# Sharing the PSUM banks out anew for the neighborhood attention of a fused two-block network

## The chip, the cores and the metric

The kernel runs on one core of one Trainium2 chip. The metric is the device time of one execution in microseconds (us); lower is better. A figure given as "the time" is the median of several executions. The trace is of one further execution, taken by the hardware profiler.

The engines are named as in the profile: PE is TensorE (matmuls and transposes), PEld its weight loads, DVE is VectorE, ACT is ScalarE, POOL is GpSimd, SP is SyncE, which here issues the DMAs. PSUM, the memory that matmuls write to, has eight banks; a tile of 128 x 512 fp32 fills one.

## The reference, cut to what matters

The network has eight stages on 256 rows of 1024 features; the change touches the fifth, the "even" layer. Half of its mixer is a long convolution (hyena), the other half neighborhood attention (NA): 16 heads of width 32, in which each query sees a window of the 4 x 64 grid and all 256 context keys in one softmax. The concatenated halves go through one 1024 x 1024 product, the mixing product.

```python
h = modulate(rmsnorm(x, g_mix), sh1, sc1)
z = h @ w_in[i]
q, k, v = jnp.split(z[..., 3 * C_HYENA:], 3, axis=-1)
...
y_na = neighborhood_attention(to_grid(q, rows), to_grid(k, rows), to_grid(v, rows), kc, vc, na_rpb[i])
y_hy = hyena_mixer(z[..., :3 * C_HYENA], *hy)
x = x + gt1 * (jnp.concatenate([y_hy, y_na], axis=-1) @ w_mix_out[i])
...
x = x + gt2 * swiglu(modulate(rmsnorm(x, g_ffn), sh2, sc2), ffn_w1[i], ffn_w3[i], ffn_w2[i])
```

## The kernel before, in words

The stages run in the order ret, ffn0, dil, ffn1, even, ffn2, fou, moe. Within them the order of instructions on each engine is set by a scheduler when the program is built: it takes whatever is ready by its own model, earlier written code first, as far as tiles are free. On the chip each engine then runs its instructions strictly in that order and waits where an operand or a tile isn't ready. PSUM tiles come from one pool with three names: `mm` for products, `tp` for transposes, `aux` for the rest. `banks(mm, tp, aux)` says how many banks each has: 4, 2, 2 in this part.

Products are made in fp32 by splitting both operands in a high and a low part (`wh`, `wl`; `xTh`, `xTl`; `yTh`, `yTl`) and adding three matmuls. `load` fetches weights by DMA (L110) into one of three raw slots and converts each half of it with one ACT instruction (L119, high part) and one DVE instruction (L120, low part) into one of five slots `w`.

**Neighborhood attention** (`neighborhood`, L915 to L945) has four column groups c of four heads; each group has two pairs of heads (h0), each pair two blocks b of 128 queries. For one head and block: two score matmuls for the local keys and two for the context keys (L936, L937) into a tile S of `aux`; DVE adds the bias and takes the extremum (L394); ACT takes the exponential (L396); DVE the reciprocal and the scaling (L398, L399); PE transposes four times into a `tp` tile (L402); ACT copies it to P (L404); the pair's 16 value matmuls (L943) add into the group's tile O. At the end of a group O is split into `yT[4 + c]` (L149, L150). For each pair the bias tables are fetched anew (L927, SP) and masked (L928, DVE).

**The mixing product** (`down`, matmuls L197) has eight weight pieces g = 0 to 7 of 12 matmuls each, 128 x 512. Piece g multiplies `yT[g]`: pieces 0 to 3 are hyena's output, 4 to 7 that of NA's column groups 0 to 3. Pieces 0 to 2 are written one by one, 3 to 7 as one block, first for the first 128 rows and then for the others. Its four result tiles take all four `mm` banks.

**Behind it** `gated_residual` multiplies the result by a row `grow`, which a DMA brings (L562), and adds x (L672, L673: DVE). Then `norm_mod` scales each block of 128 rows by its root mean square (L578, L579, L218 on POOL, L593), transposes it in two sets of four into `tp` tiles (L596), modulates them (L604 on ACT, L607 on DVE) and splits them to `xTh`, `xTl` (L149, L150). The next stage's first matmuls are L176; its constants `csrh`, `csrl` are made from a DMA (L978) into a tile `n`, of the same slots as the norm's scaled rows.

Of the kernel before, what the change touches and what calls it, by code (L numbers as in the profile page):

```python
# [24 lines left out]
PSUM = bass.MemoryType.PSUM  # L25
# [27 lines left out]
class Net:  # L53
# [24 lines left out]
    def banks(s, mm, tp, aux):  # L78

        s.psx.close()  # L80
        s.ps, s.psn = s.pool("psum%d" % mm, 1, s.psx, space=PSUM), (mm, tp, aux)

    def mm_tile(s, shape, name="mm"):
        return s.ps.tile(shape, F32, name=name, tag="mm", bufs=s.psn[0])
# [322 lines left out]
    def dilated(s, x, xt):  # L407
        nc = s.nc
        with ExitStack() as ctx:
# [24 lines left out]
            for qd in range(4):  # L434
# [45 lines left out]
                nc.sync.dma_start(out=bias.rearrange("p h k c -> p (h k) c"), in_=src)  # L480
                O = s.mm_tile([128, 2, 256])

                for c in range(2):
                    for b in range(2):
# [9 lines left out]
                        for n, (g, kb) in enumerate(order):  # L494
                            for e in range(2):
                                hs = slice(64 * (2 * c + e), 64 * (2 * c + e) + 64)
                                nc.tensor.matmul(out=O[64 * e:64 * e + 64, c, b * 128:b * 128 + 128],
                                                 lhsT=V[g][:, kb, hs], rhs=P[e][:, n, :], start=n == 0, stop=n == 3)
                for c in range(2):
                    s.split(ot[0][:, 2 * qd + c, :].rearrange("p (a s) -> p s a", s=2),  # L500
                            ot[1][:, 2 * qd + c, :].rearrange("p (a s) -> p s a", s=2),
                            O[:, c, :].rearrange("p (s a) -> p s a", s=2))
            po = s.down(ot, "attn_w_out", 0, 8)
# [411 lines left out]
    def neighborhood(s, ctx, yt):  # L915
        nc = s.nc
        p = s.pool("na", 2, ctx)
        kt, vt, mask, biases, qps = s.na
        rpb = s.a["na_rpb"]
        for c in range(4):  # L920
            O = s.mm_tile([128, 256])
            for h0 in range(0, 4, 2):
                for hh, bt in enumerate(biases, h0):
                    for r2 in range(2):
                        src = bass.AP(tensor=rpb.tensor, offset=rpb.offset + (4 * c + hh) * 1905 + (5 - r2) * 127,
                                      ap=[[1, 64], [127, 6], [1, 64]])
                        nc.sync.dma_start(out=bt[64 - 64 * r2:128 - 64 * r2, 4:10, :], in_=src)  # L927
                    nc.vector.tensor_tensor(out=bt[:, 4:10, :], in0=bt[:, 4:10, :],  # L928
                                            in1=mask[:, None, :].to_broadcast([128, 6, 64]), op=ALU.add)

                for b in range(2):
                    P = []
                    for hh, bt in enumerate(biases, h0):
                        S = s.aux_tile([128, 2, 256])
                        q = qps[c // 2][:, c % 2, hh, b * 128:b * 128 + 128]
                        nc.tensor.matmul(out=S[:, b, :], lhsT=q, rhs=kt[:, c, :], start=True, stop=True)  # L936
                        nc.tensor.matmul(out=S[:, 1 - b, :], lhsT=q, rhs=s.kc[:, c, :], start=True, stop=True)  # L937
                        P.append(s.attend(p, S.rearrange("p n c -> p (n c)"),
                                          (bt[:, 6:14, :] if b == 0 else bt[:, 0:8, :]).rearrange("p m c -> p (m c)")))
                    vs = [vt, vt, s.vc, s.vc] if b == 0 else [s.vc, s.vc, vt, vt]  # L940
                    for n in range(4):
                        for i, hh in enumerate((h0, h0 + 1)):
                            nc.tensor.matmul(out=O[32 * hh:32 * hh + 32, b * 128:b * 128 + 128],  # L943
                                             lhsT=vs[n][:, n % 2, 128 * c + 32 * hh:128 * c + 32 * hh + 32],
                                             rhs=P[i][:, n, :], start=n == 0, stop=n == 3, tile_position=(0, 32 * hh))  # L945
            s.split(yt[0][:, 4 + c, :], yt[1][:, 4 + c, :], O)

    def even_layer(s, x, xt, then):
        with ExitStack() as ctx:
            keep = s.pool("even", 1, ctx)  # L950
            yt = s.pair(keep, [128, 8, 256], "yT")
            with ExitStack() as c2:
                fill = s.neighborhood_inputs(c2, xt)
                next(fill)
                s.hyena(c2, yt, xt, fill)
                for _ in fill:
                    pass
                s.neighborhood(c2, yt)
            grow = s.mod_row(s.pool("even_g", 1, ctx), 0, 2, "grow")
            po = s.down(yt, "w_mix_out", 0, 8)  # L960
            return s.gated_residual(x, po, grow, then)

    def ffn_second(s, x, xt, then):
        with ExitStack() as ctx:
# [658 lines left out]
```

## Time and profile before

| what | value |
|---|---|
| time, median of 3 runs | 2315.85 us (2314.77 to 2316.75) |
| the profiled execution's own time | 2317.26 us |
| its span, first to last instruction | 2315.2 us |
| busy share of the span: PE, PEld, DVE, ACT | 97%, 76%, 64%, 46% |
| mean granted clock of TensorE | 0.983 of 2.4 GHz |

A window row of the trace below gives the stretch and its length in us, then for PE, PEld, DVE, ACT and POOL the busy time with the number of instructions in brackets, then PEclk (the granted clock, 1.00 is 2.4 GHz), the mean busy share of the DMA engines, and GB/s. With the instructions of one line alone, it gives PE and PEld, PEclk, DMA share and GB/s. A timeline row gives start, duration, engine, line, operation, written tile <- read tiles, shape and count, and in brackets the idle time of the engine before it and what ended that.

### The profile page before, as it was taken

The numbers are of one execution on the slowest core, as the hardware profiler recorded it, in microseconds if no ns is written. First come the engines' busy times: TensorE is split into PE (matmuls) and PEld (weight loads), VectorE is DVE, ScalarE is ACT, GpSimd is POOL, SyncE is SP. The second block draws the span as 40 slices with busy tenths as digits, with TensorE's granted clock in tenths as the row PEclk, the third lists the DMA queues.
The fourth block names the chain that finished last, engine by engine and source line by source line (L and its number), as shares of the span: only waits on it lengthen the run. The fifth ranks groups of instructions, "written<-read, shape, count | busy, mean of one in ns | idle before, by whom it ended". The sixth has DMA issues, their size and how long they took to land. (4 is left out here: it accounts for less than half of the span.)

```text
span 2315.2 us, 34156 instructions
## 1 busy us (share of the span) xinstructions
PE 2236.4 (97%) x13729; PEld 1766.7 (76%) x13729; DVE 1486.4 (64%) x2024; ACT 1072.7 (46%) x1424; POOL 33.5 (1%) x39
## 2 busy tenths in 40 slices
PE   8999999999999999998899988999999999999997
PEld 8997998899997998986699877665566656656662
DVE  6987887867746655886655457555555655555553
ACT  4333444354445444645554345544444544444442
POOL 0000000000000000100000000000000000000000
PEclk9999999999999999999999997999999999999998
DMA  8666777777743555642355627899899989998994
GB/s 308 244 255 234 264 254 273 271 263 264 268 151 132 207 191 181 217 164 40 118 189 194 254 100 278 346 414 416 356 376 425 422 338 412 425 420 356 424 424 183
DMA packets 99712, 639.75 MB, mean 276 GB/s; under 512 B 22552, under 2 KB 33433, under 8 KB 39513
## 3 DMA queue, kind: packets, MB, share of 16 engines
q1 hardware_dynamic: 99128, 636.71, 71.6%
q8 instruction: 110, 1.80, 0.3%
q10 hardware_dynamic: 416, 0.78, 0.1%
q14 instruction: 58, 0.47, 0.1%
HBM read 634.17 MB, written 3.28 MB: 275 GB/s over the span
## 5 line engine op out<-in xcount | busy, mean ns | idle before, releaser
L119 ACT ACTIVATE wh<-raw 128x1024 fp32r<-128x1024 f32 x446 | 468.8, 1059 | 552.1 <-PE mm L160 256.8
L120 DVE TENSOR_TENSOR wl<-raw,wh 128x1024 fp32r<-128x1024 f32 x446 | 538.9, 1220 | 246.4 <-ACT wh L119 245.4
L160 PE MATMUL mm<-xTh,wh 128*128 128x256 f32 x1600 | 447.5, 280 | 0.7 <-ACT tm L825 0.7
L160 PE MATMUL mm<-xTh,wl 128*128 128x256 f32 x1600 | 446.5, 279 | 0.0
L160 PE MATMUL mm<-xTl,wh 128*128 128x256 f32 x1600 | 445.3, 278 | 0.0
L120 DVE TENSOR_TENSOR wl<-rawy,wh 128x1024 fp32r<-128x1024 f32 x216 | 255.6, 1222 | 87.1 <-ACT wh L119 86.5
L160 PEld LDWEIGHTS mm<-xTh,wh 128*128 128x128 f32 x1600 | 301.3, 188 | 7.7 <-issue 5.8
L160 PEld LDWEIGHTS mm<-xTh,wl 128*128 128x128 f32 x1600 | 300.8, 188 | 4.3 <-issue 4.3
L160 PEld LDWEIGHTS mm<-xTl,wh 128*128 128x128 f32 x1600 | 301.2, 188 | 3.3 <-issue 3.3
L119 ACT ACTIVATE wh<-rawy 128x1024 fp32r<-128x1024 f32 x216 | 224.1, 1057 | 52.3 <-PE mm L1079 27.9
L1067 PE MATMUL mm<-rawx,hx 128*64 128x512 f32 x864 | 202.7, 595 | 0.0
L1079 PE MATMUL mm<-wl,hgh 128*128 128x512 f32 x448 | 179.6, 402 | 4.1 <-DVE wl L120 4.1
L1079 PE MATMUL mm<-wh,hgh 128*128 128x512 f32 x448 | 181.1, 404 | 0.0
L1079 PE MATMUL mm<-wh,hgl 128*128 128x512 f32 x448 | 177.8, 397 | 0.0
L176 PE MATMUL mm<-wh,xTh 128*128 128x256 f32 x608 | 174.1, 288 | 2.8 <-ACT wh L119 2.4
L176 PE MATMUL mm<-wh,xTl 128*128 128x256 f32 x608 | 174.3, 287 | 1.5 <-DVE xTl L150 1.5
L176 PE MATMUL mm<-wl,xTh 128*128 128x256 f32 x608 | 173.9, 286 | 0.5 <-DVE wl L120 0.5
L1067 PEld LDWEIGHTS mm<-rawx,hx 128*64 128x64 f32 x864 | 62.3, 137 | 117.8 <-issue 117.3
L535 DVE CUSTOM_DVE_ANT_0 araw<-araw,cond 128x1024 f32<-128x1024 f32 x96 | 115.7, 1218 | 33.3 <-DMA araw<-in_w_ada_dram 33.2
L176 PEld LDWEIGHTS mm<-wh,xTh 128*128 128x128 f32 x608 | 118.3, 195 | 5.1 <-ACT wh L119 2.8
L176 PEld LDWEIGHTS mm<-wh,xTl 128*128 128x128 f32 x608 | 118.7, 195 | 2.8 <-DVE xTl L150 2.3
L176 PEld LDWEIGHTS mm<-wl,xTh 128*128 128x128 f32 x608 | 118.4, 195 | 1.5 <-DVE wl L120 1.0
(361 smaller groups left out, 3293.6 us busy)
## 6 DMA issues: line engine op xcount, KB each, us to landing
rawx<-in_moe_w_dram SPq DMA_DIRECT2D x56, 2048.0 KB, 11.3
rawy<-in_moe_w_dram SPq DMA_DIRECT2D x56, 2048.0 KB, 15.0
raw<-in_moe_w_dram SPq DMA_DIRECT2D x84, 1024.0 KB, 11.5
araw<-in_w_ada_dram SPq DMA_DIRECT2D x48, 1024.0 KB, 5.5
raw<-in_ffn_w_up_dram SPq DMA_DIRECT2D x44, 1024.0 KB, 4.8
raw<-in_attn_w_in_dram SPq DMA_DIRECT2D x36, 1024.0 KB, 5.0
raw<-in_ffn_w_dram SPq DMA_DIRECT2D x33, 1024.0 KB, 4.9
x<-in_moe_w_dram SPq DMA_DIRECT2D x28, 1024.0 KB, 8.2
```

The lines of the kernel that those rows point to most:

```text
L119: nc.scalar.activation(out=h, in_=v, func=AF.Copy)
L120: nc.vector.tensor_tensor(out=l, in0=v, in1=h.bitcast(F32), op=ALU.subtract)
L160: s.nc.tensor.matmul(out=p[:, j, :], lhsT=a[:, kc, :], rhs=b[:, kc, :], start=n == 0, stop=n == 23)
L176: s.nc.tensor.matmul(out=p[:, tb if to is None else to, :], lhsT=a[:, kc, tb, :], rhs=b[:, kc % 4, :], start=n == 0, stop=n == 23)
L535: nc.vector.tensor_tensor_reduce(out=out, in0=r[:, j, :], in1=cond[src], scale=1.0, scalar=0.0, op0=ALU.mult, op1=ALU.add, accum_out=dst)
L1067: nc.tensor.matmul(out=ps[half], lhsT=x[:, kc, :], rhs=w[:, kc, :], start=kc == 0, stop=kc == 7)
L1079: nc.tensor.matmul(out=pm, lhsT=a[:, kc, :], rhs=b[:, kc % 2, :], start=n == 0, stop=n == 23)
```

## The change

NA's result tile O is taken from `aux` and no longer from `mm`. Around NA, the mixing product, the residual and the norm behind it, the banks are 4 `mm`, 1 `tp`, 3 `aux`; then they are 4, 2, 2 again. The pool has one name wherever it is opened, and a new pool's tiles wait tile by tile for the old pool's readers in the same place. Lines up to 956 keep their numbers; those behind L960 are four higher.

```diff
     def banks(s, mm, tp, aux):

         s.psx.close()
-        s.ps, s.psn = s.pool("psum%d" % mm, 1, s.psx, space=PSUM), (mm, tp, aux)
+        s.ps, s.psn = s.pool("psum", 1, s.psx, space=PSUM, reuse_waits="tile"), (mm, tp, aux)
...
         for c in range(4):
-            O = s.mm_tile([128, 256])
+            O = s.aux_tile([128, 256])
             for h0 in range(0, 4, 2):
...
                 for _ in fill:
                     pass
+
+                s.banks(4, 1, 3)
                 s.neighborhood(c2, yt)
             grow = s.mod_row(s.pool("even_g", 1, ctx), 0, 2, "grow")
             po = s.down(yt, "w_mix_out", 0, 8)
-            return s.gated_residual(x, po, grow, then)
+            x = s.gated_residual(x, po, grow, then)
+            s.banks(4, 2, 2)
+            return x
```

The scheduler turns this into another order at three places.

The first is PE at the start of NA, column group 0. `nk`, `nq`, `kc` are keys, queries and context keys, `flip` the matrix that transposes, `nv`, `vc` the values. Before:

```order
L936 MATMUL aux<-nk,nq_9905 128x256
L402 MATMUL tp<-flip,L 128x128 x4
L937 MATMUL aux<-kc,nq_9905 128x256
L402 MATMUL tp<-flip,L 128x128 x4
L943 MATMUL mm<-P,nv 32x128
L402 MATMUL tp<-flip,L 128x128 x3
L943 MATMUL mm<-P,nv 32x128 x3
```

And now:

```order
L937 MATMUL aux<-kc,nq_9905 128x256
L197 MATMUL mm<-wh,yTh 128x512 x2
L197 MATMUL mm<-wh,yTl 128x512 x2
L197 MATMUL mm<-wl,yTh 128x512 x2
L197 MATMUL mm<-wh,yTh 128x512 x2
L197 MATMUL mm<-wh,yTl 128x512 x2
L197 MATMUL mm<-wl,yTh 128x512 x2
L197 MATMUL mm<-wh,yTh 128x512 x2
L402 MATMUL tp<-flip,L 128x128 x4
L197 MATMUL mm<-wh,yTl 128x512 x2
L197 MATMUL mm<-wl,yTh 128x512 x2
L197 MATMUL mm<-wh,yTh 128x512
```

Matmuls of the mixing product stand ahead of the first head's transposes. In all, 84 of its 96 stand ahead of NA's last L943 now (17 did): 48 (pieces 0 to 3) in column group 0, 12 in each of the groups 1, 2 and 3. There is one `tp` tile: a set of four transposes can't begin before the reader of the set ahead of it is done.

The second is PE at the end of the mixing product. `ident` is the identity, `n` the scaled rows. Before:

```order
L197 MATMUL mm<-wl,yTh 128x512 x2
L596 MATMUL tp<-ident,n 128x128 x8
L1216 MATMUL aux<-wb,ones 128x64
L596 MATMUL tp<-ident,n 128x128 x4
L176 MATMUL mm<-wh,xTh 128x256
L596 MATMUL tp<-ident,n 128x128 x4
L176 MATMUL mm<-wh,xTl 128x256
```

And now:

```order
L943 MATMUL aux<-P,nv 32x128 x4
L197 MATMUL mm<-wh,yTh 128x512 x3
L197 MATMUL mm<-wh,yTl 128x512 x2
L197 MATMUL mm<-wl,yTh 128x512 x2
L197 MATMUL mm<-wh,yTh 128x512
L197 MATMUL mm<-wh,yTl 128x512 x2
L197 MATMUL mm<-wl,yTh 128x512 x2
L596 MATMUL tp<-ident,n 128x128 x16
L176 MATMUL mm<-wh,xTh 128x256
```

Twelve L197 are left behind NA, and all 16 transposes of the norm stand ahead of the next stage's first matmul, through one `tp` tile.

The third is ACT in the norm behind it. `mod` is the modulation, `tm` its result. Before:

```order
L604 ACTIVATE tm<-tp,mod 128x128 x4
L149 ACTIVATE xTh<-tm 128x4x128 x2
L149 ACTIVATE csrh<-n 128x768 x2
```

And now:

```order
L604 ACTIVATE tm<-tp,mod 128x128 x2
L149 ACTIVATE xTh<-tm 128x4x128
L149 ACTIVATE csrh<-n 128x768
L604 ACTIVATE tm<-tp,mod 128x128 x2
L149 ACTIVATE xTh<-tm 128x4x128
L604 ACTIVATE tm<-tp,mod 128x128 x2
L149 ACTIVATE csrh<-n 128x768
```

The first conversion of the next stage's constants stands ahead of the second block's L604 now. Of the conversions of weights, L119 and L120, none stood within NA; now seven pairs do, on ACT between a head's exponential (L396) and its copy (L404).

## Rows read from the trace of the kernel before

**Rows 1.** The page's first part: busy us, share of the span, instructions.

```profile
PE 2236.4 (97%) x13729; PEld 1766.7 (76%) x13729; DVE 1486.4 (64%) x2024; ACT 1072.7 (46%) x1424; POOL 33.5 (1%) x39
```

**Rows 2.** Windows: NA's four column groups, the mixing product, what follows.

```profile
1040.29:1060.96 20.67, 19.70 (x139) 13.89 (x137) 14.15 (x40) 12.29 (x27) 0.00 (x0) 1.00 0.29 71
1060.96:1082.83 21.87, 19.03 (x130) 14.05 (x129) 12.82 (x37) 10.55 (x25) 0.00 (x0) 0.92 0.20 37
1082.83:1103.01 20.18, 17.35 (x130) 12.82 (x129) 12.82 (x37) 10.56 (x25) 0.00 (x0) 1.00 0.22 41
1103.01:1124.37 21.36, 19.69 (x139) 14.27 (x138) 11.63 (x34) 10.73 (x25) 0.00 (x0) 1.00 0.11 19
1124.37:1142.52 18.15, 18.15 (x80) 14.83 (x80) 10.35 (x17) 8.90 (x13) 0.55 (x1) 1.00 0.48 167
1142.52:1151.19 8.67, 3.09 (x20) 2.87 (x19) 8.26 (x16) 5.10 (x11) 0.55 (x1) 0.76 0.74 270
```

**Rows 3.** Windows, instructions of L197 alone: NA's last group, then behind it.

```profile
1103.01:1124.37 21.36, 5.99 (x18) 3.04 (x18) 1.00 0.11 19
1124.37:1142.70 18.33, 18.31 (x79) 14.69 (x79) 1.00 0.49 169
```

**Rows 4.** Timeline of column group 2's start: one head after the other.

```profile
1084.19 0.49 DVE L399 TENSOR_SCALAR L<-L,rd 128x512 f32<-128x512 f32 x1
...
1084.82 0.63 PE L402 MATMUL tp<-flip,L 128*128 128x128 f32 x4 [0.93 <-DVE L L399]
1085.17 0.69 DVE L394 CUSTOM_DVE_ANT_0 L<-aux,nbias 128x512 f32<-128x512 f32 x1
1085.54 0.60 ACT L404 ACTIVATE P<-tp 128x512 f32<-128x512 f32 x1 [1.59 <-PE tp L402]
...
1086.04 0.71 ACT L396 ACTIVATE L<-L,nm 128x512 f32<-128x512 f32 x1
1086.19 0.41 PE L943 MATMUL mm<-P,nv 128*32 128x128 f32 x2 [0.75 <-ACT P L404]
...
1086.87 0.16 DVE L398 RECIPROCAL rd<-den 128x1 f32<-128x1 f32 x1 [0.39 <-ACT L L396]
```

**Rows 5.** Groups of instructions, 1030 to 1180 us: the conversion on DVE.

```profile
L120 DVE TENSOR_TENSOR wl<-raw,wh 128x1024 fp32r<-128x1024 f32 x23 | 27.8, 1221 | 8.0 <-ACT wh L119 8.0
```

**Rows 6.** Timeline of column group 2: two heads' transposes and their copies.

```profile
1090.32 1.10 PE L402 MATMUL tp<-flip,L 128*128 128x128 f32 x8
...
1091.07 1.08 ACT L404 ACTIVATE P<-tp 128x512 f32<-128x512 f32 x2 [1.14 <-PE tp L402]
```

**Rows 7.** Timeline from NA's end to the next stage's first matmuls (SPq issues DMAs).

```profile
1124.62 0.33 SPq L562 DMA_DIRECT2D grow<-modrows  x1
...
1135.62 1.29 DVE L672 TENSOR_TENSOR x<-mm,grow 128x512 f32<-128x512 f32 x2 [4.78 <-PE mm L197]
...
1141.63 0.88 DVE L593 TENSOR_SCALAR n<-x,rs 128x512 f32<-128x512 f32 x2 [0.73 <-POOL rs L218]
...
1147.49 0.40 DVE L607 TENSOR_SCALAR tm<-tp,mod 128x128 f32<-128x128 f32 x1
...
1149.31 1.09 PE L596 MATMUL tp<-ident,n 128*128 128x128 f32 x4 [5.58 <-DVE n L593]
...
1151.19 0.56 PE L176 MATMUL mm<-wh,xTl 128*128 128x256 f32 x1
```

**Rows 8.** DMA issues, 1000 to 1180 us: count, KB each, median us to landing.

```profile
nbias<-in_na_rpb_dram SPq DMA_DIRECT2D x28, 96.0 KB, 3.0
grow<-modrows SPq DMA_DIRECT2D x2, 512.0 KB, 3.7
n<-in_c_cs_dram SPq DMA_DIRECT2D x2, 384.0 KB
```

**Rows 9.** Operations of two tiles: csr's conversions (ns least/mean/most, stretch, shape).

```profile
L149 ACT ACTIVATE csrh<-n x2: 831/834/837, 1155.3 to 1156.0; 128x768 fp32r<-128x768 f32 x2
...
L150 DVE TENSOR_TENSOR csrl<-n,csrh x2: 952/956/959, 1156.2 to 1157.0; 128x768 fp32r<-128x768 f32 x2
```

## The prediction

> **What bounds the kernel now.** I read the busy shares first: PE is busy 97% of the span, the other engines half to two thirds [rows 1]. So what is saved or added pays where PE waits, and the windows show where that is. In NA, 1040.29 to 1124.37, 84.1 us, PE's weight loads are busy 12.8 to 14.3 us of each group's 20 to 22 [rows 2]. Holes lie in that stretch, though its matmuls look busy. In the mixing product behind it, 18.15 us, PE has no hole, and then come 8.67 us in which it is busy 3.09, until the next stage's matmuls run [rows 2].
>
> The timeline says why NA has holes. A head is a chain: bias and extremum (1085.17), exponential (1086.04, 0.87 later), reciprocal (1086.87, 0.83 later), scaling (0.2 later, an estimate from the reciprocal's 0.16), transposes 0.63 behind the scaling's start, copy 0.72 behind the transposes' start, values 0.65 behind the copy's [rows 4]. PE waits for this chain wherever it has no other head to work on. Behind the product, the gap is a chain too: residual on DVE (from 1135.62), scaling (1141.63), transposes, modulation, splits [rows 7].
>
> So two prices are to be found: what 67 moved matmuls (84 of 96 ahead of NA's end against 17) cost inside NA, and what the stretch behind NA gives back.
>
> **Behind NA.** A weight matmul takes 18.31 / 79 = 0.232 us [rows 3]. Now 12 are left: 2.8 us, and 0.4 before them for the split of O, an estimate from the copies' 0.54 for twice the columns [rows 6]. The product ends 3.2 us behind NA's end in place of 18.15: **-15.0**.
>
> That product was the cover of what follows, and it is gone. Before, the row `grow` was issued 0.25 us behind NA's end (1124.62 against 1124.37) and landed 3.7 later [rows 7, 8], long before the residual at 1135.62 asked for it. Now it is late. Counted from NA's end, in the order of DVE and PE that the change leaves:
>
> - 4.0: `grow` is there (0.25 + 3.7); the product was ready at 3.2.
> - 7.9: six operations of L672 and L673, 0.64 each (two in 1.29) [rows 7].
> - 9.3: sums and the root on POOL, 1.4, an estimate: from 1135.62 to 1141.63 lay 6.0 us, of which four such operations (2.6) and two L120 (2.4) leave 1.0 [rows 5, 7]; ACT's squares come later this time. Then L593.
> - 9.9: the first four transposes (0.44 behind the first L593, and its latency).
> - 13.2: its last reader ends. An L120 (1.22) and the second block's part stand ahead of it on DVE, 3.3 with its own modulation [rows 5, 7].
> - 14.4: the second four, which the one `tp` tile held back; at the low clock a set takes 1.09 (at 1149.31) [rows 7].
> - 18.0: only now is the first block's `n` free, and the constants' DMA into it is issued (14.5). It lands after 3.5, an estimate for 384 KB between 3.0 for 96 KB and 3.7 for 512 KB [rows 8].
> - 19.8: `csrh` (0.83) and `csrl` (0.96) [rows 9]. They stand ahead of the second block's modulation on ACT now; before, they stood behind it.
> - 20.2: modulation (0.40) [rows 7], which frees `tp` for the last set.
> - 21.0: the last transposes and the first half's split done, L176 runs on.
>
> Before it ran on at 1151.19, 26.8 behind NA's end [rows 2, 7]. So this stretch gives 26.8 - 21.0 = 5.8: -15.0 from the product, **+9.1** from a gap of 17.8 in place of 8.67. What it costs from the gap comes from three things that the product or the second `tp` tile hid: `grow` (0.8), the one `tp` tile (some 4), the constants ahead of the modulation (some 4.5).
>
> **Inside NA.** 67 x 0.232 = 15.5 us of matmuls come in. Bounds: if all fit in holes, 0; if none do, +15.5, and +3.2 for a conversion wait named below. For the weight to give this, one row is nearest: the last group held 17 such matmuls already, 3.9 us of PE, and took 21.36 against 20.18 for the group before it at full clock without any [rows 2, 3]. So 1.2 of 3.9 showed, 70% was hidden. But those had two `tp` tiles and no conversions among the heads. I walked each group along the new order with the chain's durations:
>
> - Group 0, 20.67: 48 matmuls, 11.1 us. At the starts of the two head pairs PE waits for the chain from bias to transposes, 0.87 + 0.83 + 0.2 + 0.63 = 2.5 each, so 5.1 is hidden. The conversion of a later piece stands on DVE ahead of the second pair's bias, and its slot comes free only with the last matmuls of piece 1: 3.2 of waiting for the whole chain. 20.7 + 11.1 - 5.1 + 3.2 = 29.9.
> - Group 1, 21.87, of which 1.7 (to group 2's 20.18) at a granted clock of 0.92, which I don't expect again: 12 matmuls, 2.8, of which 0.4 is hidden. 22.6.
> - Group 2, 20.18: the conversion on ACT stands ahead of a head's copy and waits for the last matmuls of an earlier piece, 1.3; at the end two heads' transposes no longer run in one go (eight in 1.10, [rows 6]): the second set waits for the first copy, 0.72 + 0.65 = 1.37 apart in place of 0.44 or so, with what follows +1.2. The 12 matmuls run within these waits. 22.7.
> - Group 3, 21.36: the same end, +1.2, and two conversions, +1.0. 23.6.
>
> Sum 98.8 against 84.1: **+14.7**. Queued behind each wait on ACT or DVE is the next head's exponential or bias, and PE waits for both: few holes of one engine are left that another fills.
>
> On the holes, the Trainium skill (Perfetto Trace Analysis, Identifying the Most-Contended Engine) holds matmul busy time for a poor measure of TensorE and goes by the weight loads' busy share; by it 29 us of the 84 are free in NA, the 15.5 fit, and the sum would be that of the first rival below. The group with 17 of them, 1.2 us longer, agrees only in part. The same page (Optimization Strategy) says that a gap which repeats can mean too little PSUM for the next tile; that speaks against taking the second `tp` bank away, and by it the ends of the groups lengthen, as the walk has it.
>
> **Other edits.** O in `aux` in place of `mm` leaves two `aux` banks for the scores, as before: nothing, unless O's group ends late, which the split at each end bounds by 0.5. The pool's name and its waits by tile cost no instruction: nothing; they are what lets the first pieces start. Seven pairs of conversions of weights move into NA; what they cost there is in the walk. Behind the gap PE is saturated, so nothing is given back later.
>
> **Sum.** +14.7 - 5.8 = +8.9. The profiled execution, 2317.26 with a span of 2315.2, would become 2326.2; the median, 1.4 lower, 2315.85 + 8.9 = **2324.8**. About 0.2% (4.6 us) is what a measurement here can tell from no change.
>
> **The rivals.**
>
> *First, faster: NA absorbs the matmuls.* If NA stays at 84.1, the sum is -5.8: 2310. For it: 6.8 to 7.8 us per group without weight loads [rows 2]. Against: the last group's 1.2 for 17, and 48 matmuls in one group hold 11.1 where 6.8 are free. It decides (faster by over 4.6) if NA grows by less than 1.2 us.
>
> *Second, no change: only group 0 grows.* The 48 cost 9.2 as walked, but groups 1 and 2 hide 70% of their 12, as the last group did of its 17 (+0.8 each), the last loses 5 (-0.4), and group 1's slow stretch is gone (-1.7): NA +8.7; sum +2.9: 2318.8. For it: 70% hidden in [rows 2, 3]. Against: the conversions and the one `tp` tile.
>
> *Third, much slower: the clock.* Group 1 ran at a granted clock of 0.92 and the gap at 0.76 [rows 2]. With more waits in NA and PE nearly idle for a gap twice as long, a clock like group 1's in two groups or their like would cost 1.7 each: +8.9 + 3.4 = +12.3: 2328, or more.
>
> *The change doesn't do what it says:* excluded; the order shows 84 of 96 ahead of NA's end.
>
> **How the numbers follow.** The walk has an error of some 3 us on each side; its own range is 2320.5 to 2328. Chances: the forecast 0.57, first rival 0.12, second 0.21, third 0.10. Forecast and third are slower by over 4.6, the second is the same, the first is faster. The range reaches down to 2312, which leaves out most of the first rival, and up to 2329, which leaves half of the third.
>
> **What would show it.** In the changed profile: NA some 99 us long, with its first group near 30 and the others at 22 to 24; the mixing product ending 3 us behind NA; then a gap near 18 us, in which DVE waits for `grow`, PE for the one `tp` tile, and the second block's modulation for the constants' DMA. I am wrong if NA grows by clearly less than its 15.5 us of new matmuls, which the last group's 30% hints at, or if the constants' DMA lands before the modulation needs ACT.

## The result: slower by 13 us

The changed kernel takes 2328.78 us (median of 4 runs, 2327.3 to 2330.66), the kernel before 2315.31 (4 runs): a ratio of 1.0058, interval 1.0046 to 1.0070. The forecast was 2324.8. The profiled execution took 2328.41 with a span of 2326.6, 11.4 more than before's. PE is busy 96% in place of 97%, the other engines as before.

The windows answer to [rows 2]: the four column groups, the product, what follows.

```profile
1039.47:1070.33 30.86, 30.75 (x187) 22.72 (x186) 19.68 (x49) 18.11 (x33) 0.00 (x0) 1.00 0.38 123
1070.33:1093.14 22.81, 20.80 (x142) 14.64 (x142) 13.95 (x37) 11.95 (x26) 0.00 (x0) 1.00 0.31 81
1093.14:1115.45 22.31, 20.59 (x141) 14.58 (x140) 13.38 (x36) 11.95 (x26) 0.00 (x0) 1.00 0.22 37
1115.45:1140.19 24.74, 19.33 (x132) 13.48 (x132) 12.20 (x34) 11.36 (x24) 0.00 (x0) 1.00 0.22 59
1140.19:1143.70 3.51, 3.03 (x13) 2.18 (x12) 0.87 (x3) 0.82 (x2) 0.00 (x0) 1.00 0.60 174
1143.70:1162.50 18.80, 4.44 (x17) 3.27 (x18) 12.25 (x26) 8.89 (x19) 1.41 (x2) 0.62 0.23 68
```

NA begins 0.8 us earlier and takes 100.7 us in place of 84.1: +16.6 (forecast +14.7). The product ends 3.5 behind it, and the gap behind the product is 18.8 in place of 8.67 (forecast 17.8). Counted as in the forecast, the next stage's second matmul stands 22.3 behind NA's end (1162.50 against 1140.19) in place of 26.8: -4.5 (forecast -5.8). The three sum to +11.3; the spans differ by 11.4. Group 1 of before ran in part at the lower clock (a granted 0.92 [rows 2]); without the 1.7 us that the prediction gives for it, NA grew by 18.3.

The first group is where most of NA's growth lies, and PE is busy there all the time. That reads as if the 48 matmuls simply took their time. The timeline of the group's start says something else. Before, PE ran the third head's scores 2.1 us into NA, ahead of the first head's transposes:

```profile
1042.37 0.70 PE L936 MATMUL aux<-nk,nq 128*128 128x256 f32 x2 [0.19 <-DVE nm L394]
...
1045.75 0.66 PE L402 MATMUL tp<-flip,L 128*128 128x128 f32 x4
```

And now PE:

```profile
1040.77 0.59 PE L937 MATMUL aux<-kc,nq 128*128 128x256 f32 x2
1041.40 0.70 PE L197 MATMUL mm<-wh,yTh 128*128 128x512 f32 x2
...
1046.35 0.39 PE L197 MATMUL mm<-wh,yTh 128*128 128x512 f32 x1
1046.58 0.60 PE L402 MATMUL tp<-flip,L 128*128 128x128 f32 x4
1047.11 0.41 PE L943 MATMUL aux<-P,nv 128*32 128x128 f32 x2
1047.44 0.70 PE L936 MATMUL aux<-nk,nq 128*128 128x256 f32 x2
```

Then DVE, and one row of ACT:

```profile
1042.61 0.68 DVE L394 CUSTOM_DVE_ANT_0 L<-aux,nbias 128x512 f32<-128x512 f32 x1
1043.22 0.69 DVE L394 CUSTOM_DVE_ANT_0 L<-aux,nbias 128x512 f32<-128x512 f32 x1
...
1048.61 0.69 DVE L394 CUSTOM_DVE_ANT_0 L<-aux,nbias 128x512 f32<-128x512 f32 x1 [1.55 <-PE aux L937]
...
1054.16 0.56 DVE L928 TENSOR_TENSOR nbias<-nbias,nmask 128x384 f32<-128x384 f32 x1 [1.23 <-DMA nbias<-in_na_rpb_dram]
1055.84 1.23 DVE L120 TENSOR_TENSOR wl<-raw,wh 128x1024 fp32r<-128x1024 f32 x1 [1.12 <-ACT wh L119]
1056.98 0.68 DVE L394 CUSTOM_DVE_ANT_0 L<-aux,nbias 128x512 f32<-128x512 f32 x1
```

```profile
1054.75 1.06 ACT L119 ACTIVATE wh<-raw 128x1024 fp32r<-128x1024 f32 x1 [0.22 <-PE mm L197]
```

DVE has taken the first two heads' scores by 1043.91 (1043.22 and 0.69), so both score banks are free before 1044. The third head's scores (1047.44, 8.0 us into NA) stand in PE's queue behind 19 matmuls of the product, two heads' transposes and the first values, and DVE takes them at 1048.61, 5.4 us after the head before. At 1055.84 a conversion stands ahead of the second pair's first head, as forecast, and waits for ACT, which waited for the product's matmuls: that head's bias table is masked by 1054.72 (L928), its bias runs at 1056.98, 2.3 later. PE is full; the heads are late.

The groups of instructions in NA show it as one number: how long ACT sat idle ahead of the exponentials. Before:

```profile
L396 ACT ACTIVATE L<-L,nm 128x512 f32<-128x512 f32 x32 | 22.8, 714 | 3.4 <-DVE rd L398 2.7 <-DVE nm L394 0.7
```

And after:

```profile
L396 ACT ACTIVATE L<-L,nm 128x512 f32<-128x512 f32 x32 | 22.9, 717 | 14.9 <-DVE nm L394 14.9
```

PE's own idle time in NA hardly changed over the same stretch: 9.1 us in brackets of its timeline against 8.0. From PE's side NA looks as dense as before. Another wait grew beside it: DVE stood 6.3 us ahead of L928 for the bias tables' DMA, against 1.0 before. It is 5.6 in e1 below, where NA takes 85.1, so it doesn't make NA long by itself.

Behind NA, the rows that answer to [rows 7], on SP, DVE, PE and ACT:

```profile
1140.37 0.33 SPq L562 DMA_DIRECT2D grow<-modrows  x1
...
1155.55 0.33 SPq L982 DMA_DIRECT2D n<-in_c_cs_dram  x1
```

```profile
1144.40 1.29 DVE L672 TENSOR_TENSOR x<-mm,grow 128x512 f32<-128x512 f32 x2 [2.32 <-DMA grow<-modrows]
...
1149.86 0.88 DVE L593 TENSOR_SCALAR n<-x,rs 128x512 f32<-128x512 f32 x2 [0.44 <-POOL rs L218]
...
1159.55 0.96 DVE L150 TENSOR_TENSOR csrl<-n,csrh 128x768 fp32r<-128x768 f32 x1
```

```profile
1150.50 1.09 PE L596 MATMUL tp<-ident,n 128*128 128x128 f32 x4 [6.80 <-DVE n L593]
1154.41 1.11 PE L596 MATMUL tp<-ident,n 128*128 128x128 f32 x4 [2.83 <-ACT tm L604]
1157.46 1.12 PE L596 MATMUL tp<-ident,n 128*128 128x128 f32 x4 [1.94 <-ACT tm L604]
1161.38 1.11 PE L596 MATMUL tp<-ident,n 128*128 128x128 f32 x4 [2.80 <-ACT tm L604]
```

```profile
1158.67 0.84 ACT L149 ACTIVATE csrh<-n 128x768 fp32r<-128x768 f32 x1 [0.60 <-DMA n<-in_c_cs_dram]
```

The steps of the forecast's list stand here, 0.2 to 1.3 us later than listed: the residual at +4.2 (4.0), the four sets at +10.3, +14.2, +17.3 and +21.2 behind NA's end (9.9, 13.3, then 20.2 for the last), and three of them wait for the modulation that reads the one `tp` tile.

### The profile page after: what moved, and what is told of

It is laid out like the page before. It is cut to its first block, busy times and chain, and to the rows that moved or that the text cites. A ratio compares the mean times of both kernels' runs of the same rounds, so it can differ in the third digit from the quotient of the medians.

```text
span 2326.6 us, 34152 instructions
## 1 busy us (share of the span) xinstructions
PE 2237.4 (96%) x13729; PEld 1764.1 (76%) x13729; DVE 1486.2 (64%) x2024; ACT 1075.5 (46%) x1424; POOL 33.7 (1%) x39
## 5 line engine op out<-in xcount | busy, mean ns | idle before, releaser
L119 ACT ACTIVATE wh<-raw 128x1024 fp32r<-128x1024 f32 x446 | 469.0, 1059 | 546.0 <-PE mm L160 258.0
L120 DVE TENSOR_TENSOR wl<-raw,wh 128x1024 fp32r<-128x1024 f32 x446 | 539.2, 1221 | 247.8 <-ACT wh L119 246.9
L120 DVE TENSOR_TENSOR wl<-rawy,wh 128x1024 fp32r<-128x1024 f32 x216 | 255.6, 1222 | 87.0 <-ACT wh L119 86.6
L119 ACT ACTIVATE wh<-rawy 128x1024 fp32r<-128x1024 f32 x216 | 224.1, 1057 | 52.2 <-PE mm L1083 27.8
```

Of the source, the lines that this page charges most:

```text
L119: nc.scalar.activation(out=h, in_=v, func=AF.Copy)
L120: nc.vector.tensor_tensor(out=l, in0=v, in1=h.bitcast(F32), op=ALU.subtract)
```

## The experiments

NA is counted from the first score matmul to the last value matmul, the gap from the product's end to the next stage's second matmul. In kernels that leave out part of the product the total time is not compared, since later stages choose experts by the values; their NA is. Each ratio is to executions of the kernel before that ran beside the kernel of its row. Each stretch is read from one traced execution. Where NA is that of the changed kernel (after, e3 to e6) and the granted clock 1.00, groups 1 and 2 agree within 0.02 us and group 0 takes 30.5 to 32.0: differences of 1.5 us in group 0 show nothing.

| run | NA | groups 0 to 3 | gap | time, ratio to before |
|---|---|---|---|---|
| before | 84.1 | 20.7, 21.9, 20.2, 21.4 | 8.7 | 2315.31 |
| after | 100.7 | 30.9, 22.8, 22.3, 24.7 | 18.8 | 2328.78, 1.0058 |
| e1 | 85.1 | 21.3, 20.2, 21.8, 21.8 | 13.4 | 2321.42, 1.0026 |
| e2 | 103.2 | 30.3, 25.7, 23.7, 23.5 | 12.4 | 2322.93, 1.0036 |
| e3 | 107.2 | 32.0, 22.8, 22.3, 30.1 | 12.1 | 2322.45, 1.0030 |
| e4 | 100.8 | 30.9, 22.8, 22.3, 24.7 | 16.8 | 2325.37, 1.0045 |
| e5 | 100.2 | 30.5, 22.8, 22.3, 24.6 | 17.9 | 2325.41, 1.0050 |
| e6 | 101.7 | 31.8, 22.8, 22.3, 24.8 | 11.8 | 2318.83, 1.0020 |
| e7 | 110.5 | 32.1, 26.4, 24.4, 27.7 | - | - |
| e8 | 100.5 | 35.1, 21.9, 21.9, 21.6 | - | - |
| e9 | 101.7 | 31.0, 22.8, 22.3, 25.6 | - | - |
| e10 | 94.0 | 25.5, 23.8, 24.1, 20.5 | 10.2 | 2312.35, 0.9984 |
| e11 | 103.1 | 28.0, 27.5, 24.1, 23.4 | 15.9 | 2327.85, 1.0058 |
| e12 | 102.0 | 27.9, 23.4, 24.7, 26.0 | - | - |

### What NA costs

**e1, one `tp` bank alone.** O stays in `mm`, so the product starts late as before.

```diff
-            O = s.aux_tile([128, 256])
+            O = s.mm_tile([128, 256])
```

> The kernel before with the new banks (4, 1, 3) around NA and the norm, but O left in mm, so that the mixing product starts late as before (25 of its 96 matmuls inside NA, 17 before). NA is counted from the first score matmul to the last value matmul: 84.1 us before, 100.7 after. Theory A, each matmul that moves into NA costs its own 0.23 us of PE there and the single tp bank and the conversions cost at most 2 us: NA 86 us (84.1 + 8 x 0.23), the gap behind the product some 13 to 14 us through the single tp bank and the constants, time about 2320. Theory B, NA grew through the single tp bank and the conversions on ACT and DVE that the heads wait for: NA 90 us or more though hardly a matmul moved, time 2324 or more.

Theory A holds. NA took 85.1: one `tp` bank in place of two, with eight more matmuls and three banks for the scores, costs NA some 1 us, or 2.7 when before's slow stretch (1.7) is taken off. Most of what it costs lies behind the product: the gap grew from 8.7 to 13.4. The interval of the time is 1.0017 to 1.0036.

**e2, two `tp` banks, one `aux` bank for scores.**

```diff
-                s.banks(4, 1, 3)
+                s.banks(4, 2, 2)
```

> The changed kernel with banks (4, 2, 2): O in aux, two tp banks kept, one aux bank for scores; 84 of 96 matmuls stay inside NA. Theory A: NA stays at 99 to 102 us, since only some 2 us of PE's idle time there ends at a transpose's tile; the norm behind gains some 4 us from its second tp bank: time 2323 to 2327. Theory B: NA falls to 95 us or less, time 2320 or less.

NA 103.2, 2.5 longer than after, beyond both theories: whatever the second `tp` bank gives in NA, the missing score bank costs more. The gap fell from 18.8 to 12.4, and with it the time (1.0026 to 1.0046).

**e7 and e8, matmuls left out.** The first 48 (e7) or 84 (e8) matmuls of the product are not issued; hyena's half, or seven eighths, of the product is missing. The cut below is e7's; e8 has 7 in place of 4.

```diff
+        first = 4 if name == "w_mix_out" else 0
...
                     for g in fs:
+                        if g < first:
+                            continue
                         wh, wl = w[g]
```

> The changed kernel without the 48 matmuls of the mixing product's pieces 0 to 3 (hyena's half of the product is left out); their weights are still fetched and converted, and the single tp bank stays. Theory A: NA falls by 48 x 0.23 = 11.1 us to about 89.6, all of it in the first column group. Theory B: the conversions and the tp bank keep NA at 96 us or more.

> The changed kernel without the 84 matmuls of pieces 0 to 6 (only the last eighth of the mixing product is computed), so NA has the single tp bank but no matmul of the product. Theory A: NA falls by 84 x 0.23 = 19.5 us to 81 us, below the 84.1 of before, which held 17 of them. Theory B: NA stays at 90 us or more.

NA did not fall: it is 110.5 and 100.5 without the matmuls. But neither run is a clean test of theory A, nor settles more by its first group, for two things changed beside the matmuls. With the weight slots free at once, conversions moved to NA's start, ahead of the heads; and the clock fell in parts of e7's groups 0, 1 and 3 (a granted 0.89, 0.94 and 0.79) and of e8's first group, where PE once stood idle for 8.48 us:

```profile
1040.49:1075.60 35.11, 22.71 (x138) 15.48 (x136) 23.34 (x51) 19.86 (x36) 0.00 (x0) 0.85 0.55 177
1075.60:1097.51 21.91, 18.17 (x129) 12.67 (x128) 12.83 (x38) 11.00 (x25) 0.00 (x0) 1.00 0.19 37
1097.51:1119.43 21.92, 18.18 (x129) 12.68 (x128) 12.84 (x38) 11.00 (x25) 0.00 (x0) 1.00 0.21 37
```

Groups 1 to 3 of e8 are clean, without a conversion or a matmul of the product at a granted 1.00: 21.9, 21.9, 21.6. Before's one undisturbed group without such matmuls, group 2, took 20.2. So the new sharing of banks alone, one `tp` bank and O among the scores, costs groups 1 and 2 some 1.7 us each. In e1, with one `tp` bank and O left in `mm`, they took 20.2 and 21.8.

**e9, the same matmuls made short.** The 48 write 128 columns in place of 512 (`first` is 4, as in e7) and their result is overwritten, which leaves out hyena's half. The order of instructions is the changed kernel's.

```diff
+                                n = 128 if g < first else 512
...
-                                                   rhs=b[:, 0, c * 512:c * 512 + 512],
+                                                   rhs=b[:, 0, c * 512:c * 512 + n],
...
```

> The changed kernel, in which the 48 matmuls of pieces 0 to 3 write 128 columns in place of 512 (the rest of hyena's half of the product is left out); the order of instructions and all conversions stay. Theory A, the first column group (30.9 us) is long through these matmuls' own time on PE: a matmul of 128 columns takes some 0.11 in place of 0.23, so the group falls by 5 to 6 us to about 25. Theory B, the four conversions of weights that now stand among its heads, and the score banks, set its length: 29 us or more, with idle time on PE where the matmuls shrank.

The first group took 31.0, at a granted clock of 0.94:

```profile
1036.11:1067.13 31.02, 27.27 (x187) 21.09 (x186) 19.46 (x48) 18.10 (x33) 0.00 (x0) 0.94 0.39 131
```

Even if the clock's missing 6% is taken as 1.9 us (an estimate: 0.06 of 31.02), some 2 of the 5.9 us that were taken from PE's work show, which is little more than group 0's scatter (5.9 is an estimate: 48 times 0.23 less 0.11; two short matmuls take 0.23 together). The first head pair, with 24 of the 48, ends 18.1 us into NA (16.65 in the changed kernel), 16.5 if its missing clock of 0.09 is taken off: hardly earlier. PE now waits openly for a head, with all the matmuls ahead of it done:

```profile
1042.07 0.66 PE L406 MATMUL tp<-flip,L 128*128 128x128 f32 x4 [1.77 <-DVE L L403]
```

Theory B holds: the matmuls' own time is not what makes the group long. The third head's scores start 8.7 us into NA here too, behind the first two heads' transposes and first values.

**e12, no conversions in the first group.** Pieces 4 to 7 use the weights of 0 to 3 again; the lower half of the weight matrix is left out.

```diff
-                w += s.load(s.unit_r(name, base + f // 2))
+                w += w[f - 4:f - 2] if f >= 4 and name == "w_mix_out" else s.load(s.unit_r(name, base + f // 2))
```

> The changed kernel, in which pieces 4 to 7 of the mixing product use the weights of pieces 0 to 3 again (the lower half of the weight matrix is left out), so that no conversion of weights stands among the heads of column group 0 any more; all 96 matmuls stay, 48 of them in group 0, and the third head's scores still stand behind 20 of them and behind the first values. Theory A, the conversions' waits set group 0's length: it falls from 30.9 us to 26 or less. Theory B, PE's order sets it (a head's scores behind the product's matmuls and the values of the heads before): 29 us or more. Between the two: both share in it.

27.9, between the two. The first head pair ends 16.0 us into NA, near after's 16.65 (before 11.76), and the second pair is 2.3 us faster (11.9 against 14.2). But 37 of the product's matmuls stand in the group and not 48, ten of the missing eleven in the second pair, so this run alone doesn't part them from the conversions. The changed kernel's own rows do: there the second pair's first bias ran 2.3 us late, behind the conversion (1054.72 to 1056.98 above), and in e12 it follows its L928 at once. So the conversions cost some 2.3 us, 3 at most; the first pair's delay is left to the order. The third head's bias waits for its scores here too:

```profile
1043.50 0.69 DVE L394 CUSTOM_DVE_ANT_0 L<-aux,nbias 128x512 f32<-128x512 f32 x1 [2.81 <-PE aux L937]
```

### What the stretch behind NA costs

**e3, the norm's tiles from `aux`.** Three banks in place of one; a flag is set around `gated_residual`.

```diff
-            pt = s.tp_tile([128, 4, 128])
+            pt = (s.aux_tile if s.norm_aux else s.tp_tile)([128, 4, 128])
```

> The changed kernel, with the transposes' tiles of the norm behind the mixing product taken from the three aux banks in place of the one tp bank; NA is untouched. Theory A, the longer gap comes from the one tp tile above all: of the waits 2.83, 1.94 and 2.80 us ahead of the second to fourth set, 6 to 7 us go, the next stage runs on 15 to 16 us behind NA's end in place of 22.3, time about 2322. Theory B, grow and the constants set the end and the tile's wait moves to them: 1 to 2 us go, time about 2327.

Theory A holds: the gap fell by 6.7, and the sets run in twos. NA of this execution was long by a slow stretch of the clock in its last group (below). The interval of the time is 1.0017 to 1.0042.

```profile
1152.93 1.97 PE L597 MATMUL aux<-ident,n 128*128 128x128 f32 x8 [4.82 <-DVE n L594]
1156.27 1.94 PE L597 MATMUL aux<-ident,n 128*128 128x128 f32 x8 [1.38 <-DVE n L594]
```

```profile
1148.11:1160.16 12.05, 4.29 (x17) 3.52 (x18) 11.31 (x26) 8.37 (x20) 1.41 (x2) 0.58 0.32 93
```

**e4, `grow` ahead of NA.**

```diff
             yt = s.pair(keep, [128, 8, 256], "yT")
+            grow = s.mod_row(s.pool("even_g", 1, ctx), 0, 2, "grow")
...
-            grow = s.mod_row(s.pool("even_g", 1, ctx), 0, 2, "grow")
```

> The changed kernel, with grow fetched ahead of NA. Theory A: the residual starts when the product's first block is done, some 1 us earlier (2 at most), and the whole chain with it: time 2327 to 2328. Theory B, grow is hidden by the product's last matmuls anyway: no change, 2328.8.

The gap fell by 2.0, the most that theory A allowed. The residual begins 2.2 behind NA's end, when the first block of the product is done.

```profile
1141.70:1158.51 16.81, 4.45 (x18) 3.28 (x18) 11.22 (x26) 8.83 (x19) 1.41 (x2) 0.58 0.21 68
```

**e5, the constants behind the next stage's first half**, through the weights' raw slots.

```diff
-            cr = s.np.tile([128, D], F32, name="n")
...
+            s.fill_constants()
             po = s.down(ht, "ffn_w2", 0, 22)
```

> The changed kernel, with the next stage's constants fetched and converted through the weights' raw slots behind that stage's first half, so that they leave the norm. Theory A: the last set of transposes no longer waits for csrh (0.84, and 0.60 for its DMA) and csrl (0.96): 2 us go, time about 2326.8. Theory B, the second block's modulation waits for the one tp tile as long without them: under 0.5 us go, time 2328.5.

The gap fell by 0.95, half of what theory A had.

```profile
1143.63:1161.48 17.85, 4.45 (x18) 3.28 (x18) 11.37 (x25) 8.16 (x18) 1.41 (x2) 0.59 0.11 39
```

The last set's wait fell from 2.80 to 1.93 and stayed with the one `tp` tile. The times of e4 and e5 (1.0028 to 1.0061, 1.0033 to 1.0067) overlap with the changed kernel's, so the trace alone tells here.

**e6, the three together.**

> The three edits together: the norm's tiles from aux, grow ahead of NA, the constants later; NA as in the changed kernel. Theory A: the gap falls by 8 to 9 us, to about what it was before the change, time about 2320; what is left against 2315 is NA's growth less the product's 15 us. If the tail were all of the loss, the time would be 2315 or less.

The gap fell by 7.0, to 11.8, where theory A had 8 to 9: the parts don't add up (6.7, 2.0, 0.95). A wait that one edit removes is in part taken over by another, as in e5, where the last set's stayed with the one `tp` tile. The time is 1.0020, 1.0010 to 1.0030: with most of the gap's growth gone the kernel is still slower, by what NA lost.

```profile
1143.15:1154.90 11.75, 4.29 (x18) 3.52 (x18) 10.61 (x27) 7.69 (x19) 1.41 (x2) 0.66 0.12 45
```

### A version that beats both

**e10 and e11, O in the halves of one bank of its own**, on top of e6; with one `tp` and two score banks (e10), or two and one (e11).

```diff
+        Os = s.ps.tile([128, 2, 256], F32, name="o", tag="o", bufs=1)
         for c in range(4):
-            O = s.aux_tile([128, 256])
+            O = Os[:, c % 2, :]
...
-                s.banks(4, 1, 3)
+                s.banks(4, 1, 2)
```

> The kernel with the three edits behind NA, and O in the two halves of one bank of its own, so that the scores keep two aux banks at every moment (4 mm, 1 tp, 2 aux, 1 for O). The order now weaves the product's matmuls in by ones and twos over the groups 0 and 1. Theory A, PE's own time bounds NA: it stays at 100 to 102 us, time 2317 to 2319. Theory B, NA lost to an order in which heads have too few score banks to run ahead: NA 93 to 97 us, time 2310 to 2315, no slower than before the change.

> As the run before, but with two tp banks and one aux bank for scores. Theory A: NA 100 to 103, time 2317 to 2320. Theory B: one score bank leaves every head's scores waiting for the head before, NA 103 us or more, time 2320 or more.

e10 takes 2312.35, 0.9984 of before (0.9975 to 0.9993): faster, by less than 0.2%. Theory B holds. NA took 94.0 with the same 84 matmuls inside, 7.7 less than e6, whose stretch behind NA has the same edits. Its groups:

```profile
1036.79:1062.31 25.52, 24.17 (x160) 17.82 (x159) 15.87 (x43) 14.50 (x30) 0.00 (x0) 1.00 0.37 99
1062.31:1086.15 23.84, 23.84 (x157) 17.28 (x156) 14.05 (x37) 12.43 (x25) 0.00 (x0) 1.00 0.29 78
1086.15:1110.21 24.06, 24.00 (x157) 17.54 (x156) 16.73 (x41) 14.09 (x30) 0.00 (x0) 1.00 0.31 78
1110.21:1130.75 20.54, 17.65 (x129) 12.83 (x128) 11.59 (x34) 11.24 (x24) 0.00 (x0) 1.00 0.26 71
```

The banks and, with them, the scheduler's order changed together here; neither was changed alone. In this order the scores run ahead: one matmul of the product stands between the second and the third head, and the third head's scores start 3.5 us into NA, not 8.0. PE waits there for a score bank, not the heads for PE.

```profile
1038.34 0.58 PE L198 MATMUL mm<-wh,yTh 128*128 128x512 f32 x1
1040.27 0.70 PE L938 MATMUL aux<-nk,nq 128*128 128x256 f32 x2 [1.35 <-DVE nm L395]
```

```profile
L397 ACT ACTIVATE L<-L,nm 128x512 f32<-128x512 f32 x32 | 22.9, 715 | 6.1 <-DVE nm L395 4.2 <-DVE rd L399 1.8
```

ACT's idle time ahead of the exponentials is 6.1 us, against 14.9 in the changed kernel. e11, with one bank for scores, took 103.1 in NA and 2327.85, as theory B had it. Its norm still waits for single tiles, since `aux` has one bank there too.

## Why the prediction was right, and where its steps were not

**Slower, by NA's growth less what the stretch behind gives back: right.** NA's +16.6 and the stretch's -4.5 stand where the sum had +14.7 and -5.8. Both errors point the same way, and the time came out 4.0 above the forecast, above the walk's own range (2320.5 to 2328) and just under the wide one's end (2329).

**Group 0, 20.7 to 29.9: the size was right (30.9), the reason only in part.** The step counted the 48 matmuls' 11.1 us on PE, less 5.1 hidden, plus 3.2 for a conversion. The conversion's part is there: 2.3, 3 at most. The rest is hardly PE's time: with three quarters of the columns taken away some 2 us went (e9). What the rows show in its place is the scores' place in PE's queue. A head's chain on DVE and ACT starts only when its scores have run, and the order put the third head's behind the first two heads' transposes and first values, 8.0 us into NA in place of 2.1; the matmuls fill the wait. That the step's total fits is luck. No run changes that order alone, so its share is what e9 and e12 leave over, and not a measured one. Why the scheduler leaves the scores back here and not in e10, where they also have two banks, stays open.

**Groups 1 and 2: the sizes were right** (22.8 and 22.3 against 22.6 and 22.7), **group 1's by luck.** The step let 2.4 of its matmuls' 2.8 us show and gave the banks nothing. In e8 the sharing of banks costs 1.7 in each of these groups even without matmuls or conversions, so the 12 matmuls and a conversion together show with 0.4 to 0.9 (22.8 and 22.3 against 21.9). The matmuls are hidden to two thirds or more, as the last group before [rows 2, 3] had it. In group 2 the walk had hidden them, and priced waits of 2.5 for the one `tp` tile and a conversion. **Group 3: 1.1 too low** (24.7 against 23.6), though it held one conversion and not the walk's two; DVE waits 2.02 us there for a bias table's DMA, which the walk didn't have.

**O in `aux`, priced at nothing or 0.5 at most: wrong.** With O in a bank of its own and the same matmuls inside, NA is 7.7 us shorter (e10 against e6), in the other order that comes with it.

**The stretch behind NA: the sum was 1.3 off, its split wrong.** The term for the one `tp` tile was 4 and is 6.7 (e3) where taken alone. The constants' term was 4.5 and is 0.95 (e5): the list left out the third set of transposes, whose wait for the one `tp` tile runs while the constants are fetched, and goes on without them. `grow` was priced at 0.8 from the product's end; it is 2.0 (e4), since the residual needs only the first block.

**The rivals.** The first (NA absorbs the matmuls) fell: NA grew by 16.6. With other banks (e10) the 67 matmuls (15.5 us) lengthen NA by 9.9, or 11.6 without before's slow stretch, so a quarter to a third is hidden; that kernel is faster because its gap is short too (10.2). The second rival had the matmuls of groups 1 and 2 right, and lacked the 1.7 in each for the shared banks. The Trainium skill (Perfetto Trace Analysis, Identifying the Most-Contended Engine) judges TensorE's headroom by the share of peak FLOPs and the weight loads' busy share. By the second NA had 29 us free before, and 35 of 100.7 after. Of such headroom e10's order uses a part, and the changed kernel's on balance none: the share tells nothing of whether the order lets a matmul use it. The same page's rule on repeating gaps and too little PSUM (Optimization Strategy) agrees in part: in NA PE stands idle for 10.2 and 10.3 us with one score bank (e2 and e11), and for 4.3 with two at every moment (e10); but before and after the change, where NA grew by 16.6, it is 8.3 and 9.3 (each a length less its busy time). The third rival, the clock, did not occur in NA in the profiled execution of the changed kernel, whose groups ran at a granted 1.00, and the gap's lower clock (0.62) was in the forecast's list; that its 2328 lies nearest to the measured time is an accident. In one group of e3 it did occur.

## What to carry to other kernels

Filling an engine's idle time with other work paid here only where the filler stood behind the instructions that feed the other engines' chains. So read the idle time of the engines that are fed as well (here ACT ahead of the exponentials: 3.4 us before, 14.9 after, 6.1 in e10), not only that of the engine that is filled. It tells a good order from a bad one and is no measure of the loss: in e11 it is 10.2, and NA is longer than in the changed kernel. When a stretch of solid work is moved away, list what it covered (here a DMA, a shared tile and a conversion), and expect the waits to replace one another and not to add up. Try a long-lived accumulator in PSUM of its own, and not in a share of the banks that a pipeline turns over, as long as the pipeline keeps two banks (94.0 in e10; with one, in e11, 103.1).

## What was not expected of the hardware

A slow stretch of TensorE's clock comes in one execution and not in another of the same order in NA: there is none in the changed kernel, e4, e5 and e6, and one in group 3 of e3, a mean of 0.77. (Before had one in group 1, 0.92 [rows 2].) It cost 5.3 us there (30.06 against 24.74):

```profile
1113.17:1143.23 30.06, 23.83 (x133) 16.17 (x132) 12.19 (x34) 11.36 (x24) 0.00 (x0) 0.77 0.21 49
```

From about 1129.4 us to the group's end PE ran at the lower level, 1.2 GHz: four transposes took up to 1.12 us and not 0.66. Just before, PE had waited 1.08 us for a score bank, where it waited 0.21 in the changed kernel; that this decides it is not shown. The 5.3 us are more than the 4.6 that a median can tell here, so stretches were compared by windows with their granted clock, and times by medians.
